# Who waits for the last store, and when: SyncE ahead of the engines' first meeting, or GpSimd after it

## The chip, the cores and the metric

The kernel runs on one core of a Trainium2 chip. The rounds of experiments ran on different chips (numbers 0, 5 and 14), so each ratio compares runs of one round alone. The time is device time in microseconds (us), and lower is better; the median of several executions is quoted. A profile belongs to one of these executions. Its span runs from the first to the last instruction of the program; what lies around the program is outside the span but inside the time (122.94 us of time for a span of 121.2 in the profiled run of the kernel before). After the program's last instruction the trace of that run has further semaphore updates: nine of semaphore 2 (121.389 to 121.914 us from the start of the span), a sweep over many others (121.813 to 122.479), and nine more of semaphore 2 (122.704 to 123.061). No instruction record names semaphore 2, so I put these updates down to the runtime, call semaphore 2 the runtime's and each group of nine a barrier; the names are mine.

## The reference

Two arrays of 1024 x 4096 floats are added, and GELU (in its tanh form) is taken of the sum:

```python
z = x + y
return (0.5 * z * (1 + np.tanh(np.sqrt(2 / np.pi) * (z + 0.044715 * z ** 3)))).astype(np.float32)
```

33.55 MB are read and 16.78 MB written: 50.3 MB for one pass of cheap arithmetic.

## The kernel before

The data lie on 128 partitions, 32768 floats on each. All ten loads and five stores are issued from SyncE's queue, the last two stores being half as large as the others (16 KB per partition). GpSimd adds, ScalarE and VectorE do the rest, in chunks of 1024 columns.

```python
    loads = [2048, 6144, 8192, 8192, 8192]
    stores = [8192, 8192, 8192, 4096, 4096]
    ...
    def store(i):
        a, b = sr[i]
        nc.sync.dma_start(out=ov[:, a:b], in_=zt[:, a:b])
    ...
    ctx.close()
    tc.close()
    tc.compile()
    begin_early(nc, 2)
```

The end that this case is about is not in the source: the framework adds it. It is the third block of the program, and its order is this (my summary of its instructions):

```
SyncE    drain: wait for all semaphores of the program (stores, loads, engines)
all      first meeting: four engines report (drain, semaphore 96 + 1);
         GpSimd waits for four reports, then lets them go (semaphore 97 + 4)
GpSimd   drain, clear of the program's semaphores 99 to 109
all      second meeting, like the first
```

In the trace instructions wait for a semaphore's value and change it: SyncE's drain at 120.466 us waits for semaphore 97 and raises 96, whose update follows at 120.474. Drains carry waits and reports here. ScalarE's first report, a drain, starts 6 ns after its last activation does (102.064 and 102.058 us), lasts 1.04 us and ends 35 ns after that activation (103.101 and 103.066); a later one lasts 14 ns. I call it a meeting when all engines report and are let go together. I count a transfer as landed at the 16th update of its semaphore: the last store makes 16, from 119.280 to 120.264 us, and SyncE's wait for it passes 17 ns after the last of them.

As I read this order, the first meeting is there so that no engine still needs a semaphore when they are cleared; the second, so that no engine leaves before they are. (`begin_early` moves the first two loads into the program's first block; both kernels have it.) SyncE's ten waits lie on six instructions in the trace, five semaphore instructions with one or two waits each and a drain with one. Semaphore 108 counts the last store (and one earlier load; its final value is 32).

Of the kernel before, what the change touches and what calls it, by code (L numbers as in the profile page):

```python
# [1 line left out]

# [1 line left out]

# [4 lines left out]


def begin_early(nc, count):


    blocks = nc.main_func.blocks
    head, body = blocks[0], blocks[1]
    SP = mybir.EngineType.SP
    queue = [i for i in body.instructions if i.engine == SP]
    moved = [i for i in queue if isinstance(i, mybir.InstDMACopy)][:count]
    assert not any(i.sync_info and i.sync_info.on_wait for i in moved)
    at = next(k for k, i in enumerate(head.instructions) if i.engine == SP and isinstance(i, mybir.InstDrain))  # L20
    for k, i in enumerate(moved):
        body.instructions.remove(i)
        head.instructions.insert(at + k, i)


@with_exitstack
def kernel(
    ctx: ExitStack,
    tc: tile.TileContext,
    x: bass.AP,  # L30
    y: bass.AP,
    out: bass.AP,
):








    nc = tc.nc
    P = nc.NUM_PARTITIONS
    fp32 = mybir.dt.float32
    act = mybir.ActivationFunctionType
    alu = mybir.AluOpType

    N, D = x.shape
    assert N % P == 0
    TOT = N // P * D  # L50
    xv, yv, ov = (a.rearrange("(p n) d -> p (n d)", p=P) for a in (x, y, out))

    c1 = 2.0 * math.sqrt(2.0 / math.pi)
    root = math.sqrt(c1 * 0.044715)

    YS = 8192
    CH = 1024
    PS = 4
    loads = [2048, 6144, 8192, 8192, 8192]
    stores = [8192, 8192, 8192, 4096, 4096]  # L60

    def ranges(sizes):
        ends = [sum(sizes[: i + 1]) for i in range(len(sizes))]
        assert ends[-1] == TOT
        return [(e - f, e) for e, f in zip(ends, sizes)]

    lr, sr, cr = ranges(loads), ranges(stores), ranges([CH] * (TOT // CH))
    C = len(cr)
    by_pool = set(range(1, C))

    def over(rs, lo, hi):
        return [i for i, (a, b) in enumerate(rs) if a < hi and b > lo]

    pool_sb = ctx.enter_context(tc.tile_pool(name="xz", bufs=1))
    pool_y = ctx.enter_context(tc.tile_pool(name="y", bufs=2))
    pool_w = ctx.enter_context(
        tc.tile_pool(name="w", bufs=PS, space=bass.MemoryType.PSUM)
    )

    zt = pool_sb.tile([P, TOT], fp32, tag="z", name="z")  # L80
    yt, wt = {}, {}

    def load_x(i):
        a, b = lr[i]
        nc.sync.dma_start(out=zt[:, a:b], in_=xv[:, a:b])  # L85

    def load_y(i):
        a, b = lr[i]
        s, o = divmod(a, YS)
        if o == 0:  # L90
            yt[s] = pool_y.tile([P, YS], fp32, tag="y", name=f"y{s}")
        nc.sync.dma_start(out=yt[s][:, o : o + b - a], in_=yv[:, a:b])  # L92
# [5 lines that stand above are left out]
    def add(c):  # L98
        a, b = cr[c]
        s, o = divmod(a, YS)  # L100
        eng = nc.gpsimd if c in by_pool else nc.vector
        eng.tensor_add(out=zt[:, a:b], in0=zt[:, a:b], in1=yt[s][:, o : o + b - a])  # L102

    def sq(c):
        a, b = cr[c]
        wt[c] = pool_w.tile([P, CH], fp32, tag="w", name=f"w{c}")
        nc.scalar.activation(  # L107
            out=wt[c], in_=zt[:, a:b], func=act.Square, scale=root
        )

    def stt(c):
        a, b = cr[c]
        nc.vector.scalar_tensor_tensor(  # L113
            out=wt[c], in0=wt[c], scalar=c1, in1=zt[:, a:b], op0=alu.add, op1=alu.mult
        )

    def sig(c):
        nc.scalar.activation(out=wt[c], in_=wt[c], func=act.Sigmoid)  # L118

    def mul(c):  # L120
        a, b = cr[c]
        nc.vector.tensor_mul(out=zt[:, a:b], in0=wt[c], in1=zt[:, a:b])  # L122


    sp = []
    for i in range(len(loads)):
        sp += [(load_x, i), (load_y, i)]
    sp += [(store, i) for i in range(len(stores))]
    pool = [(add, c) for c in range(C) if c in by_pool]
    dve, acts = [], []  # L130
    for i in range(-3, C + 1):
        if 0 <= i < C:
            dve.append((stt, i))
            acts.append((sig, i))
        if 0 <= i - 1 < C:
            dve.append((mul, i - 1))
        if 0 <= i + 3 < C and i + 3 not in by_pool:
            dve.append((add, i + 3))
        if 0 <= i + 2 < C:
            acts.append((sq, i + 2))  # L140

    needs = {
        load_x: lambda i: [],
        load_y: lambda i: [
            (add, c)
            for c in over(cr, lr[i][0] - 2 * YS, lr[i][0] - YS)
            if lr[i][0] % YS == 0
        ],
        add: lambda c: [(f, i) for i in over(lr, *cr[c]) for f in (load_x, load_y)],
        sq: lambda c: [(add, c)] + ([(mul, c - PS)] if c >= PS else []),  # L150
        stt: lambda c: [(sq, c)],
        sig: lambda c: [(stt, c)],
        mul: lambda c: [(sig, c)],
        store: lambda i: [(mul, c) for c in over(cr, *sr[i])],
    }
    queues = [sp, pool, acts, dve]
    done = set()
    with tc.manual_schedule():
        one = pool_sb.tile([P, 1], fp32, tag="one", name="one")
        nc.vector.memset(one, 0.0)  # L160
        nc.scalar.activation(out=one, in_=one, func=act.Sigmoid)  # L161
        while any(queues):
            moved = False
            for q in queues:
                while q and all(n in done for n in needs[q[0][0]](q[0][1])):
                    fn, arg = q.pop(0)
                    fn(arg)
                    done.add((fn, arg))
                    moved = True
                    if q is not sp:  # L170
                        break
            assert moved, [q[:1] for q in queues]

    ctx.close()
    tc.close()
    tc.compile()
    begin_early(nc, 2)


# [1 line left out]
_INS = ['x', 'y']  # L181
_OUTS = [((1024, 4096), 'float32')]


# [23 lines left out]
```

## Time and profile before

| | before |
|---|---|
| time, median (6 runs) | 122.67 us (122.49 to 123.08) |
| span of the profiled run | 121.2 us |
| transfers, mean over the span | 416 GB/s, 97.8% of 16 engines' time |
| last arithmetic ends | 104.3 us |
| last store, issue to landing | 15.91 us |

The first part of the page of the kernel before gives each engine's busy time, its share of the span and its number of instructions:

```profile
DVE 75.5 (62%) x66; ACT 63.8 (53%) x66; POOL 73.0 (60%) x35
```

No compute engine is busy for more than 62% of the span, while the transfer queue holds its 16 engines for 97.8% of it. The bound is memory traffic. What a change of the end can gain lies after the last store's landing. For that the page is too coarse, so the single records of instructions and semaphore updates are used below; they were read from the packed trace itself, since no view prints them, and have three decimals.

### The profile page before, as it was taken

To read this page: it belongs to the slowest core of one execution; us is meant where nothing else is said; L and a number is where in the kernel's file an instruction comes from. 1 tells how busy PE (TensorE), PEld (TensorE's weight loads), DVE (VectorE), ACT (ScalarE), POOL (GpSimd) and SP (SyncE) were. 2 spreads that over 40 slices of the span, in tenths; PEclk is the share of its full clock that TensorE was granted. 3 is DMA by queue.
4 is the path that set the end of the run, shared out by engine and by line. 5 is a ranking of instruction groups with operands and counts; after the bars stand their busy time and mean duration, and the time that the engine had idled before them with its cause. 6 is when DMAs were issued, how large, how long until landed. Compare 5 with 4: busy or idle time off the path is not lost.

```text
span 121.2 us, 248 instructions
## 1 busy us (share of the span) xinstructions
DVE 75.5 (62%) x66; ACT 63.8 (53%) x66; POOL 73.0 (60%) x35
## 2 busy tenths in 40 slices
DVE  0044700059999019999997999994999999400000
ACT  4016200078875047888858878874878878000000
POOL 0056000699980299999889999949999990000000
DMA  6999999999999989898989898998999999989992
GB/s 197 417 468 422 471 406 433 476 389 476 389 476 389 476 379 487 357 508 357 508 346 519 346 519 346 346 487 381 479 389 476 389 476 389 487 379 411 433 433 108
DMA packets 2162, 50.35 MB, mean 416 GB/s; under 512 B 240, under 2 KB 240, under 8 KB 240
## 3 DMA queue, kind: packets, MB, share of 16 engines
q1 hardware_dynamic: 2160, 50.33, 97.8%
q14 instruction: 2, 0.02, 0.0%
HBM read 33.55 MB, written 16.78 MB: 415 GB/s over the span
## 4 chain that ended last, share of the span: by engine, by line
DMA 49%; POOL 17%; DVE 16%; SPq 1%; ACT 1%; issue 0%; POOLq 0%
DMA y<-in_y_dram 49%; POOL z L102 17%; DVE z L122 8%; DVE w L113 8%; ACT w L107 1%; SPq L85 1%; SPq L92 1%; POOLq L102 0%
## 5 line engine op out<-in xcount | busy, mean ns | idle before, releaser
L102 POOL TENSOR_TENSOR z<-z,y 128x1024 f32<-128x1024 f32 x31 | 72.8, 2388 | 26.5 <-DMA y<-in_y_dram 26.5
L113 DVE SCALAR_TENSOR_TENSOR w<-w,z 128x1024 f32<-128x1024 f32 x32 | 39.4, 1232 | 21.4 <-ACT w L107 21.4
L107 ACT ACTIVATE w<-z 128x1024 f32<-128x1024 f32 x32 | 32.9, 1028 | 37.7 <-POOL z L102 31.7
L122 DVE TENSOR_TENSOR z<-w,z 128x1024 f32<-128x1024 f32 x32 | 38.8, 1214 | 0.0
L118 ACT ACTIVATE w<-w 128x1024 f32<-128x1024 f32 x32 | 31.4, 981 | 0.4 <-DVE w L113 0.4
L102 DVE TENSOR_TENSOR z<-z,y 128x1024 f32<-128x1024 f32 x1 | 1.2, 1224 | 6.1 <-DMA y<-in_y_dram 6.1
L161 ACT ACT_TABLE_LOAD x1 | 1.3, 1283 | 1.3 <-PEq L192 1.3
L160 DVE MEMSET one<- 128x1 f32 x1 | 0.1, 59 | 1.3 <-PEq L192 1.3
L192 POOL MEMSET const-float32-0.0<- 128x1 f32 x1 | 0.1, 99 | 0.2 <-issue 0.2
L161 ACT ACTIVATE one<-one 128x1 f32<-128x1 f32 x1 | 0.2, 203 | 0.0
L192 POOL MEMSET const-bfloat16-1.0<- 128x1 bf16 x1 | 0.1, 102 | 0.0
L192 POOL MEMSET const-uint8-127<- 128x1 uint8 x1 | 0.1, 102 | 0.0
L192 POOL MEMSET const-float32-1.0<- 128x1 f32 x1 | 0.1, 99 | 0.0
## 6 DMA issues: line engine op xcount, KB each, us to landing
z<-in_x_dram SPq DMA_DIRECT2D x3, 4096.0 KB, 34.2
y<-in_y_dram SPq DMA_DIRECT2D x3, 4096.0 KB, 24.8
out_dram<-z SPq DMA_DIRECT2D x3, 4096.0 KB, 30.8
out_dram<-z SPq DMA_DIRECT2D x2, 2048.0 KB, 17.5
z<-in_x_dram SPq DMA_DIRECT2D x1, 3072.0 KB, 13.4
y<-in_y_dram SPq DMA_DIRECT2D x1, 3072.0 KB, 20.4
z<-in_x_dram SPq DMA_DIRECT2D x1, 1024.0 KB, 4.9
y<-in_y_dram SPq DMA_DIRECT2D x1, 1024.0 KB, 6.9
```

The costliest lines, as they stand in the source:

```text
L85: nc.sync.dma_start(out=zt[:, a:b], in_=xv[:, a:b])
L92: nc.sync.dma_start(out=yt[s][:, o : o + b - a], in_=yv[:, a:b])
L102: eng.tensor_add(out=zt[:, a:b], in0=zt[:, a:b], in1=yt[s][:, o : o + b - a])
L107: nc.scalar.activation(out=wt[c], in_=zt[:, a:b], func=act.Square, scale=root)
L113: nc.vector.scalar_tensor_tensor(out=wt[c], in0=wt[c], scalar=c1, in1=zt[:, a:b], op0=alu.add, op1=alu.mult)
L118: nc.scalar.activation(out=wt[c], in_=wt[c], func=act.Sigmoid)
L122: nc.vector.tensor_mul(out=zt[:, a:b], in0=wt[c], in1=zt[:, a:b])
L160: nc.vector.memset(one, 0.0)
L161: nc.scalar.activation(out=one, in_=one, func=act.Sigmoid)
L192: nc = _bacc.Bacc("TRN2", target_bir_lowering=False, num_devices=1)
```

## The change

SyncE no longer waits for the last store ahead of the first meeting. The meeting then takes place while that store is under way, and GpSimd waits for the store afterwards, in the drain with which the clearing begins. The point is that the meeting does not need the store; only the clearing and the program's end do.

```diff
+def wait_late(nc):
+    body, end = nc.main_func.blocks[1:3]
+    SP, POOL = mybir.EngineType.SP, mybir.EngineType.Pool
+    last = [i for i in body.instructions if isinstance(i, mybir.InstDMACopy)][-1]
+    (sem,) = [u.id for u in last.sync_info.on_update]
+    all_done = end.instructions[0]
+    clear = next(i for i in end.instructions if isinstance(i, mybir.InstDrain) and i.is_reset_sema)
     ... (assertions)
+    waits = all_done.sync_info.on_wait
+    its = [w for w in waits if w.id == sem]
+    rest = [w for w in waits if w.id != sem]
+
+    def drain(old, waits, **reset):
+        return mybir.InstDrain(
+            name=old.name, engine=old.engine, debug=old.debug,
+            sync_info=mybir.SyncInfo(on_wait=waits, on_update=[]), **reset
+        )
+
+    at = end.instructions.index(clear)
+    end.instructions[0] = drain(all_done, rest, is_reset_sema=False)
+    end.instructions[at] = drain(
+        clear, its, is_reset_sema=True,
+        reset_range_start=clear.reset_range_start, reset_range_stop=clear.reset_range_stop,
+    )
 ...
     tc.compile()
     begin_early(nc, 2)
+    wait_late(nc)
```

More of the change, by code (lines that the diff above doesn't have):

```diff
@@ L23, in begin_early @@
         head.instructions.insert(at + k, i)
+def wait_late(nc):
[5 more added lines that the diff above has]
+    clear = next(i for i in end.instructions if isinstance(i, mybir.InstDrain) and i.is_reset_sema)
+    assert all_done.engine == SP and clear.engine == POOL and clear.sync_info is None
+    waits = all_done.sync_info.on_wait
+    its = [w for w in waits if w.id == sem]
+    assert len(its) == 1
+    rest = [w for w in waits if w.id != sem]
[10 more added lines that the diff above has]
+    )
 @with_exitstack
```

## The prediction

The sum came to 393 - 24 = 369 ns, all read off the trace of the kernel before, and so to 122.65 - 0.37 = 122.28 us.

> **What bounds the kernel now.** I read four views, from coarse to fine. First the page's slices of the span, to see what is at work when.
>
> ```profile
> DVE  0044700059999019999997999994999999400000
> ACT  4016200078875047888858878874878878000000
> POOL 0056000699980299999889999949999990000000
> DMA  6999999999999989898989898998999999989992
> GB/s 197 417 468 422 471 406 433 476 389 476 389 476 389 476 379 487 357 508 357 508 346 519 346 519 346 346 487 381 479 389 476 389 476 389 487 379 411 433 433 108
> ```
>
> The transfers are under way from the first slice to the last but one; the three compute engines are idle in the last five to seven slices (3.0 us each). So memory traffic bounds the kernel, and its end is set by the last store and whatever comes after it. The page's chain of work that ended last is of no use for this end: it follows arithmetic alone and stops with the last DVE multiply, at 104.3 us.
>
> Second, the windows view (busy time and transfer by stretch), over the last 2.2 us:
>
> ```profile
> 119.00:119.50 0.50, 0.00 (x0) 0.00 (x0) 0.00 (x0) 1.00 0.09 33
> 119.50:120.00 0.50, 0.00 (x0) 0.00 (x0) 0.00 (x0) 1.00 0.00 0
> 120.00:120.30 0.30, 0.00 (x0) 0.00 (x0) 0.00 (x0) 1.00 0.00 0
> 120.30:120.70 0.40, 0.00 (x0) 0.00 (x0) 0.00 (x0) 1.00 0.00 0
> 120.70:121.20 0.50, 0.00 (x0) 0.00 (x0) 0.00 (x0) 1.00 0.00 0
> ```
>
> The last two columns are the transfer share and GB/s, counted at a packet's start. No packet starts after 119.5 us, yet the span runs to 121.15: 1.6 us of end, in which neither data nor arithmetic is started.
>
> Third, the waits of the SyncE queue (total, times, longest):
>
> ```profile
> SPq L176 <- DMA out_dram<-z: 15.4, 3, 5.9
> SPq L176 <- PEq L176: 0.6, 2, 0.4
> ```
>
> Line 176 stands for everything the framework adds around the program. There SyncE waits three times for stores, 15.4 us in all: these are the last three stores, one after the other. What SyncE does after the third of those waits is the matter of the change.
>
> Fourth, line 176 alone, for GpSimd and for SyncE, from 120.3 and 104.7 us on (duration in ns min/median/max, first and last start):
>
> ```profile
> L176 POOLq EVENT_SEMAPHORE  x4: 17/17/17, 120.5 to 121.0; - x4
> L176 POOLq DRAIN  x2: 34/58/83, 120.7 to 120.9; - x2
> L176 POOLq EVENT_SEMAPHORE_RANGE_CLEAR  x1: 95/95/95, 120.8 to 120.8; - x1
> ...
> L176 SPq EVENT_SEMAPHORE  x7: 17/28/28, 104.7 to 121.1; - x7
> L176 SPq DRAIN  x3: 7/7/7, 120.4 to 120.7; - x3
> ```
>
> All four GpSimd semaphore instructions, both its drains and the clear fall after the last store. The individual records and semaphore updates behind these rows, to the nanosecond, give the order:
>
> | us | what |
> |---|---|
> | 115.437 | 16th update of the fourth store's semaphore |
> | 120.264 | 16th update of the last store's semaphore |
> | 120.281 | SyncE: wait for it and one older semaphore passes |
> | 120.342 | SyncE: next pair of waits, long fulfilled |
> | 120.407 | SyncE: the drain with the last wait, long fulfilled |
> | 120.466 | SyncE: drain that reports to the first meeting |
> | 120.498 | GpSimd: has seen all reports |
> | 120.576 | GpSimd: lets the others go |
> | 120.657 | GpSimd: drain (83 ns), first of the clearing |
> | 120.769 | GpSimd: clear of the semaphore range (95 ns) |
> | 120.893 | GpSimd: drain (34 ns) |
> | 120.971, 121.050 | GpSimd: second meeting, seen and let go |
> | 121.091 to 121.154 | the four other engines pass it; end of the span |
>
> So the end splits in three: last data packet over (119.887) to the semaphore's 16th update, 0.377 us; that update to GpSimd's first clearing drain, 120.657 - 120.264 = **0.393 us**; that drain to the end of the span, 121.154 - 120.657 = **0.497 us**.
>
> [...] SyncE's wait record is 28 ns long and starts 17 ns after the 16th update, though SyncE had stood there since 115.5 us. Hence I work from start to start, not with durations: the seven records from 120.281 to 120.657 last 7 to 83 ns, but their starts lie 32 to 81 ns apart. [...] The trace has 16 updates for the last store, from 119.280 to 120.264; whoever waits, GpSimd or SyncE, must wait for the one at 120.264. [...] The trace has updates of semaphore 2 from 121.389 on and a sweep of resets up to 122.48, all after the second meeting, so they should follow it as it moves.
>
> **The change part by part.**
>
> *Removed from SyncE:* the wait for the last store. Its remaining waits end with the fourth store's, at 115.437. Before, it took 120.466 - 120.264 = 0.202 us from the update to the report; after an equal sequence it reports near 115.437 + 0.2 = 115.64 (one pair of waits may fall away, 0.06 us). The other engines' reports are older: ACT's drain is at 102.06, DVE's at 103.11, its update at 104.39. GpSimd lets everyone go about 0.15 us later, near 115.8, and the four others report to the second meeting some 0.2 us after that (before: let go at 120.60, last report at 120.80), near 116.0. All this is 4.2 us ahead of the last store's landing, so all of it is hidden.
>
> *Moved to GpSimd:* the one wait, onto the first drain of the clearing. GpSimd will have stood there since about 115.9. It answers a semaphore that it has long waited for in 120.498 - 120.474 = 24 ns (its first-meeting wait in the kernel before, from update to start). So the drain starts at 120.264 + 0.024 = 120.288 instead of 120.657.
>
> *Unchanged:* drain, clear, drain, second meeting: 0.497 us. In the kernel before GpSimd was itself the last at the second meeting: the others' last report came at 120.801, while GpSimd's own second drain ended at 120.927. Earlier reports therefore gain nothing more there.
>
> Sum on the path: starts that leave it 17 + 61 + 65 + 59 + 32 + 78 + 81 = 393 ns; wait that comes onto it 24 ns; difference **0.369 us**. New span 121.154 - 0.369 = 120.785 us. The measured time has a further part around the span (122.94 against 121.2 in the profiled run) that I take to move along unchanged: 122.65 - 0.37 = **122.28 us**, 0.30% less.
>
> **The rivals.** *A: the wait costs an instruction more on GpSimd.* If the wait becomes a semaphore instruction of its own ahead of the drain, the path gets one more start-to-start step, 0.08 us by GpSimd's own (120.498 to 120.576 to 120.657). For it: SyncE's many waits were split into instructions of at most two. Against: SyncE's last drain carries one wait itself (120.407), and here too there is one wait. It would make 122.36. *B: nothing is gained, because something else already fills these 0.37 us,* such as the runtime's end work waiting for a transfer rather than for the engines. For it: the trace ends its program part at 121.154, and I can't see what the runtime waits for. Against: its first semaphore update comes 0.22 us after the second meeting's last, in an unbroken sequence. It would make 122.65. *C: more is gained, because the second meeting shrinks as well,* down to the full 0.89 us between landing and end of span. For it: the other engines arrive early. Against: 120.801 is before 120.927, GpSimd was the last anyway, and the clear can't start before the store has landed. With everything gone it would make 121.76, still within 2%[...]. *D: the store lands later,* because SyncE or the meeting disturbs it. Against: these are a few semaphore updates at 115.6 to 116.0 beside 433 GB/s, and the kernel before passes like updates at 104.39 and 110.6. No change of time that I could name.
>
> **Range and chances.** The three runs before lie within 0.20 us (122.49 to 122.69), and transfers set the time, so a median of a new session may lie 0.1 to 0.25 us off without any change. The gain has a narrow range by itself (0.29 with rival A to 0.39). Both together: 121.98 to 122.57 for 8 in 10; this leaves B's 122.65 just outside, to which I give one chance in ten. Two per cent is 2.45 us, while the whole end after the landing, all that a rearrangement of the engines could remove, is 0.89 us: faster by over 2% 0.005, slower 0.005, within 0.99.
>
> **What would show each step.** In the changed kernel's records: (i) SyncE's report to the first meeting and GpSimd's letting go lie 4 us or more before the last store's 16th update, near 115.6 and 115.8; (ii) GpSimd's 83 ns drain starts within 30 ns of that update (about 0.1 with rival A); (iii) from that drain to the end of the span 0.49 to 0.50 us; (iv) from the update to the end of the span 0.52 us instead of 0.89; (v) the store takes 15.9 us from issue to landing, as before. The prediction would be wrong if (ii) shows over 0.1 us, if (iii) has grown (GpSimd slower after a wait), or if all five hold and the time still doesn't fall by 0.3 to 0.4 us against runs of the kernel before on the same chip: then the rest of the time doesn't move with the span.

## The result

The changed kernel takes 122.27 us (median of 6 runs, 121.96 to 122.44) against 122.67 us. The ratio is 0.9963, with a 95% interval of 0.9942 to 0.9984. Ratios here are the mean time of one kernel's runs over that of the other's of the same rounds, so not quite the ratio of the medians that I quote. The interval leaves out 1, so there is a small gain.

**The profile after.** The transfer lines of its slices (40 equal slices of the span; busy share in tenths, then GB/s):

```profile
DMA  6999999989898989898989899999999999998994
GB/s 201 430 457 449 440 416 446 468 381 489 348 522 348 522 348 522 348 511 359 500 370 489 381 478 391 359 402 459 394 468 402 468 402 468 391 478 364 430 435 174
```

The picture is the same up to the last slice, which now is 4 tenths full instead of 2: the idle end is a smaller part of it. The windows view of the changed kernel over its last 1.5 us (start and end, length, busy time of VectorE, ScalarE and GpSimd, clock, transfer share, GB/s):

```profile
119.00:119.50 0.50, 0.00 (x0) 0.00 (x0) 0.00 (x0) 1.00 0.08 33
119.50:120.00 0.50, 0.00 (x0) 0.00 (x0) 0.00 (x0) 1.00 0.00 0
120.00:120.30 0.30, 0.00 (x0) 0.00 (x0) 0.00 (x0) 1.00 0.00 0
120.30:120.53 0.23, 0.00 (x0) 0.00 (x0) 0.00 (x0) 1.00 0.00 0
```

As before, no packet of data starts after 119.5 us (the trace has a packet of 4 bytes at 119.629, and before two at 119.523 and 119.883, which the view shows as 0 GB/s and the prediction left out); but the span ends at 120.53 instead of 121.15. The waits of SyncE's queue (total, times, longest), where line 205 of this kernel is line 176 of the one before:

```profile
SPq L205 <- DMA out_dram<-z: 10.6, 2, 5.8
SPq L205 <- PEq L205: 5.0, 2, 4.9
```

SyncE waits for two stores instead of three. In place of the third wait (4.8 us) stands a wait of 4.9 us for other engines: SyncE now spends the last store's time standing at the second meeting. Line 205 in the changed kernel, first GpSimd from 115.0 to 115.6 us, then GpSimd from 119.5 us on, then SyncE from 104.3 us on:

```profile
L205 POOLq EVENT_SEMAPHORE  x2: 17/17/17, 115.4 to 115.5; - x2
...
L205 POOLq DRAIN  x2: 34/58/83, 120.0 to 120.3; - x2
L205 POOLq EVENT_SEMAPHORE  x2: 17/17/17, 120.4 to 120.4; - x2
L205 POOLq EVENT_SEMAPHORE_RANGE_CLEAR  x1: 95/95/95, 120.1 to 120.1; - x1
...
L205 SPq EVENT_SEMAPHORE  x6: 17/28/28, 104.6 to 120.5; - x6
L205 SPq DRAIN  x3: 7/7/7, 115.3 to 115.6; - x3
```

GpSimd's four semaphore instructions, which all stood behind the last store, have come apart: the first meeting's two lie at 115.4 and 115.5 us, the second's two at 120.4. SyncE's three drains have gone from 120.4 to 120.7 us to 115.3 to 115.6. The durations are the same. One of SyncE's semaphore instructions is gone, because the nine waits left lie on five instructions, two on each of four and one on the drain, where the ten lay on six.

The single records of the two traces side by side (us from the start of each span):

| event | before | after |
|---|---|---|
| fourth store, 16th update | 115.437 | 115.193 |
| SyncE reports to the first meeting | 120.466 | 115.396 |
| GpSimd lets the others go | 120.576 | 115.507 |
| last store, 16th update | 120.264 | 120.013 |
| GpSimd's first clearing drain starts | 120.657 | 120.037 |
| end of the span | 121.154 | 120.534 |
| last update of the runtime's semaphore 2 | 123.061 | 122.442 |
| last store's update to that drain | 0.393 | 0.024 |
| that drain to the end of the span | 0.497 | 0.497 |
| end of the span to the runtime's last update | 1.907 | 1.908 |

Where the 0.620 us between the two spans came from: 0.369 us from the distance between the landing and the drain, nothing from what follows, and the remaining 0.251 us because the store landed earlier in this execution. Of these, 0.244 us were there already when the fourth store landed (115.193 against 115.437), ahead of the first meeting and with all stores issued, so they are hardly the change's. Several of the experiments bear on it.

### The profile page after: what moved, and what is told of

Same layout as the page of the kernel before. It is cut to its first block, busy times and chain, and to the rows that moved or that the text cites. A ratio compares the mean times of both kernels' runs of the same rounds, so it can differ in the third digit from the quotient of the medians.

```text
span 120.5 us, 247 instructions
## 1 busy us (share of the span) xinstructions
DVE 75.5 (63%) x66; ACT 63.8 (53%) x66; POOL 73.0 (61%) x35
## 4 chain that ended last, share of the span: by engine, by line
DMA 49%; POOL 17%; DVE 16%; SPq 1%; ACT 1%; issue 0%; POOLq 0%
DMA y<-in_y_dram 49%; POOL z L131 17%; DVE z L151 8%; DVE w L142 8%; ACT w L136 1%; SPq L114 1%; SPq L121 0%; POOLq L131 0%
```

## The experiments

My theory is the prediction's: between the last store's 16th semaphore update and the end of the span, the starts of instructions that follow each other add up one by one, and what is moved ahead of that update is free. The rivals: it counts who waits and not when the meeting is held; the store itself lands earlier or later; something beside the engines' end sets the time.

All of these kernels gave correct results. Their edits are shown shortened, with parts in words. The distance from the last store's 16th update to the end of the span is called **the tail** from here on. It was 0.890 us before and 0.521 us after, and it comes from one profile of each kernel. The scatter of the runs, about 0.2 us either way, comes mostly from elsewhere, as the comparison further down shows.

### Only the order of SyncE's waits

```diff
     waits = old.sync_info.on_wait
+    waits = [w for w in waits if w.id == sem] + [w for w in waits if w.id != sem]
```

(The first wait of the list ends up in the drain itself, the last of SyncE's six instructions.)

> SyncE still waits for all stores ahead of the first meeting, but for the last one last of all, in the drain that carries one wait itself. Theory (only starts between the last store's 16th semaphore update and the end of the span count): two starts of 61 and 65 ns leave that path, so update to end of span falls from 0.890 to 0.764 us and the time by 0.13 us, about a third of the change's gain. Rival 1 (the gain needs the store to be waited for after the meeting; the order of waits is nothing): 0.89 us and no gain. Rival 2 (the changed kernel gained because its store landed earlier, 120.01 against 120.26 us in its profile): update to end as the theory has it, but the landing moves in step with the number of SyncE's waits, so here as in the kernel before, near 120.26.

Measured: tail **0.764 us** (119.949 to 120.713), time 122.45 against 122.61 us, ratio 0.9986 (0.9965 to 1.0008). SyncE's waits and its records from 119 us on:

```profile
SPq L190 <- DMA out_dram<-z: 15.3, 3, 5.8
...
L190 SPq DRAIN  x3: 7/7/7, 120.0 to 120.3; - x3
L190 SPq EVENT_SEMAPHORE  x2: 17/17/17, 120.2 to 120.7; - x2
```

SyncE still waits for three stores. After the landing there are only drains, reports and the meetings' own semaphore instructions; the two instructions with waits long fulfilled that stood there before, the pair at 120.342 and the drain's own at 120.407, no longer follow the last store's wait, which the drain now carries. The tail is the theory's, to the nanosecond, so rival 1 falls: 0.126 of the 0.369 us have nothing to do with when the meeting is held. They are two instructions whose waits were fulfilled and that happened to stand behind the last store's. The landing is 0.32 us earlier than in the kernel before although SyncE has the same number of waits, which speaks against rival 2; it is one execution of each, and the comparison further down has more on it. The time's interval includes both 0 and 0.13 us; the timer alone would not have told.

### GpSimd waits, but ahead of the first meeting

```diff
+    end.instructions[0] = drain(old, rest)      # SyncE: without the last store's
+    end.instructions[at] = drain(first, its)    # GpSimd's drain ahead of the first meeting
```

> GpSimd instead of SyncE waits for the last store, but ahead of the first meeting, so the meeting still comes after the landing. Theory: SyncE's report (0.202 us after the update) leaves the path; GpSimd's answer to the store (24 ns), one more start-to-start step of GpSimd (78 to 112 ns), its release (78) and the step to the clearing drain (81) stay: 0.26 to 0.30 us from the update to that drain instead of 0.393, update to end of span 0.76 to 0.79, time 0.10 to 0.13 us less. Rival 1 (it is who waits that counts, not when the meeting is): update to end near 0.52 and the whole gain of 0.37.

Measured: tail **0.759 us** (119.732 to 120.491), time 122.44 against 122.61 us, ratio 0.9984 (0.9962 to 1.0007). GpSimd's records from 119.5 to 120.06 us:

```profile
L202 POOLq DRAIN  x2: 41/59/77, 119.8 to 120.0; - x2
L202 POOLq EVENT_SEMAPHORE  x2: 17/17/17, 119.8 to 119.9; - x2
```

GpSimd's drain starts 24 ns after the update, as in the changed kernel; its semaphore instruction follows 85 ns later (41 ns drain), the release 78 ns after that, the clearing drain 81 ns after that. Having GpSimd wait is worth 0.131 us (of which 6 ns are a clearing drain of 77 instead of 83 ns) and not 0.369. The other 0.238 us of the change come from holding the meeting before the landing.

### One meeting more, before and after the change

```diff
+    meeting = list(end.instructions)[1:at]      # the 11 instructions of the first meeting
+    for k, i in enumerate(meeting):
+        end.instructions.insert(at + k, <a copy of i under a new name>)
```

> The kernel before with the first meeting held twice. Theory: after the first release the others report at up to 144 ns later than GpSimd's drain starts, so GpSimd sees the reports of the added meeting 0.33 us after the first's (120.825 for 120.498): update to end of span 1.22 us instead of 0.89, time 0.33 us more. Rival (what the engines do at the end is hidden beside something else that ends the timed run): no change of the time though the span grows.

> The changed kernel with the first meeting held twice. Theory: the added 0.33 us lies beside the store, from about 115.4 us on, and costs nothing: update to end of span stays 0.52 us, time as the changed kernel (0.37 us under the kernel before). Rival (meetings cost wherever they stand, for instance by disturbing the store): 0.33 us of the gain is lost, so nearly the time of the kernel before, or the store lands later by a like amount.

Measured, before with three meetings: tail **1.212 us**, that is 0.322 us more; time 122.70 against 122.61 us, ratio 1.0005 (0.9987 to 1.0024). After with three meetings: tail **0.515 us**; time 122.16 against 122.61 us, ratio 0.9958 (0.9940 to 0.9975).

The tails are as expected (the clearing drain took 77 instead of 83 ns, which is the 6 ns in both). The time of the first is not: 0.33 us more were expected, and the interval ends at 0.29. Either its executions happened to have early landings, or the meetings don't count in full. So the dose was raised.

### Eight meetings more

The same edit with the copied meeting eight times.

> The kernel before with the first meeting held nine times (ten meetings in all). One added meeting took 0.322 us more from landing to end of span in its profile, but its timed runs showed only about 0.1 us, within their scatter; eight added ones are out of the scatter. Theory: 8 x 0.328 = 2.62 us more on the path, update to end of span 3.51 us, time near 125.25 us. Rival (the time is bound by something beside the engines' end, and the meetings are partly hidden): the span grows, the time by less than half of 2.62.

> The changed kernel with the same eight added meetings. Theory: they end near 115.6 + 2.6 = 118.2 us, 1.8 us ahead of the last store's landing, so update to end of span stays 0.515 us and the time stays near 122.25. Rival (meetings disturb the store, or cost wherever they stand): the store's 15.8 us from issue to landing, or the time, grows by a good part of 2.6 us.

Measured, before with ten meetings: tail 3.804 us, 2.914 more than before; time 125.88 against 122.81 us, ratio 1.0252 (1.0235 to 1.0268). After with ten meetings: tail **0.519 us**; time 122.47 against 122.81 us, ratio 0.9976 (0.9960 to 0.9992). The records of GpSimd from 120.3 us on in the first:

```profile
L196 POOLq EVENT_SEMAPHORE  x20: 17/17/17, 120.6 to 124.0; - x20
L196 POOLq DRAIN  x10: 34/34/77, 120.7 to 123.9; - x10
L196 POOLq EVENT_SEMAPHORE_RANGE_CLEAR  x1: 95/95/95, 123.8 to 123.8; - x1
```

and in the second, first from 115.0 to 118.6 us, then from 119.9 us on:

```profile
L225 POOLq EVENT_SEMAPHORE  x18: 17/17/17, 115.5 to 118.5; - x18
L225 POOLq DRAIN  x8: 34/34/41, 115.6 to 118.2; - x8
...
L225 POOLq DRAIN  x2: 34/56/77, 120.1 to 120.3; - x2
L225 POOLq EVENT_SEMAPHORE  x2: 17/17/17, 120.4 to 120.5; - x2
L225 POOLq EVENT_SEMAPHORE_RANGE_CLEAR  x1: 93/93/93, 120.2 to 120.2; - x1
```

These are the same instructions. In the one kernel all twenty semaphore instructions stand behind the landing (120.343 us) and the clear comes at 123.8; in the other, eighteen stand beside the store and the clear comes at 120.2, as if they weren't there. The time follows: the first takes 3.07 us more than the kernel before (difference of the medians), the second is still 0.34 us below it. Its store took 15.78 us from issue to landing, so eight meetings beside it did not slow it. So the engines' end counts in full. That run's missing 0.24 us (0.09 measured for 0.33) lie within the span: the record has the span of each execution to 0.1 us, and time less span is 1.8 us there as in the kernel before, while the median spans are 120.9 and 121.0 us. Nothing is hidden in the runtime's part. Earlier landings in those executions would explain it; their landings are not on record. The profiled one, at 123.02 us, was the slowest of the six.

The tail came out 0.29 us longer than expected in the first kernel. Seven of the eight meetings took 0.327 to 0.367 us from start to start; one took 0.575, and it was the seventh added one in all three of the long kernels. In that one the last report came at 122.885 us and GpSimd started 271 ns later instead of 24. The long kernels have one more packet in their instruction queue; here the one made from the kernel before (packets, MB, share of 16 engines' span):

```profile
q14 instruction: 3, 0.02, 0.1%
```

It was 2 before. It would be tempting to say that GpSimd waited for that packet, but the trace speaks against it: the packet starts at 123.831 us, 0.675 us after GpSimd had gone on (123.156), and in the two longer forms of the changed kernel 1.0 and 1.4 us after the slow meeting. What GpSimd waited for stays open.

### More meetings than fit

The changed kernel with twenty meetings added, in one execution.

> The changed kernel with twenty added meetings, more than fit beside the store. Theory (GpSimd's clearing starts at the later of two times: the landing, and the end of the meetings): the meetings end at 115.59 + 20 x 0.328 = 122.15 us, 2.1 us after a landing at 120.0; update to end of span 2.6 us, time near 124.4. Rival (the clearing only waits for the store, or the time doesn't follow): time near 122.3, or up by all of 6.6 us.

Measured: tail 2.938 us, time 125.22 us. The clear, from GpSimd's records after the landing:

```profile
L225 POOLq EVENT_SEMAPHORE_RANGE_CLEAR  x1: 96/96/96, 122.8 to 122.8; - x1
```

GpSimd's clearing drain starts at 122.680 us, though the store had landed at 120.240: the meetings had not ended before. Expected were 122.15 us for the drain and a tail of 2.6. The drain is 0.53 us late: 0.17 because the stores ran later here (SyncE's report at 115.568 instead of 115.396), 0.25 from the slow seventh meeting, and about 0.1 from three of 0.36 us instead of 0.33. The time is 0.8 us over the expected 124.4: 0.34 from the tail, 0.24 from the later landing, and about 0.26 that no recorded update accounts for (see the comparison of times below). The rule holds for the drain, its size was a little low: the clearing starts at the later of two times, the landing and the end of the meetings, and what can be hidden is limited to the 4.4 us between GpSimd's being ready and the landing (115.59 to 120.01 in the changed kernel).

### Everything but one wait ahead of the landing

If a meeting that doesn't need the store is free beside it (tail 0.519 us with eight more of them, 0.521 with none), so should be the second meeting and the clearing of all semaphores but one. The next kernel does that. The clear covers semaphores 99 to 107; GpSimd takes 16 off semaphore 109 with a semaphore instruction; both meetings are held; and the last instruction of the whole program waits for the store's semaphore to be 32 and subtracts 32 in the same instruction.

```diff
+    end.instructions[0] = drain(all_done, rest, is_reset_sema=False)       # without the last store
+    end.instructions[at] = drain(clear, [], is_reset_sema=True, reset_range_start=lo, reset_range_stop=sem)
+    end.instructions[at + 1] = shorter                                     # clear of 99 to 107
+    end.instructions.insert(at + 2, wait_and_take_off("I-9000", POOL, above[0]))   # 109
     ... second meeting, unchanged
+    end.instructions.append(wait_and_take_off("I-9100", <engine>, its[0])) # 108, the last store
```

> A step further than the change: all semaphores but the last store's are cleared, and the second meeting is held, while the store is under way; at the very end GpSimd alone waits for the store and subtracts its 32 in the same instruction. Theory: 24 ns to GpSimd's answer and 17 ns of it are left in the program, 0.04 us instead of 0.521; if the runtime's 1.907 us after the span follow as one piece, update to the last of the runtime's semaphore updates 1.95 us instead of 2.43, time 0.48 us under the changed kernel and 0.85 under before, near 121.8. Rival 1 (the other engines, already in the runtime's own barrier, have part of it done): still less, as much as 0.2 to 0.5 us. Rival 2 (the runtime waits by other means for transfers or for all engines' records): no gain over the changed kernel.

Measured: tail **0.041 us**, time 121.84 against 122.81 us, ratio 0.9932 (0.9914 to 0.9950). By the ratio that is 0.84 us under before, where 0.85 was expected. From the landing to the runtime's last update it took 2.037 us instead of the 1.95 expected (2.429 after the change), so rival 2 falls. The program's part is as the theory has it; the runtime's part grew from 1.908 to 1.996 us. The updates of the runtime's semaphore 2 say why:

| kernel | first of its barriers after the program, updates in us |
|---|---|
| after | 120.769, 120.803, **121.008**, 121.052, 121.075, then four up to 121.294 |
| all ahead, GpSimd last | 116.417, 116.451, **120.617**, 120.662, 120.685, then four up to 120.903 |

Two updates come while the store is still under way, the third only after GpSimd is done. So the updates are a chain, and GpSimd is third in it. In both kernels the third update comes 0.561 us after the end of GpSimd's last instruction (120.447 and 120.056 us). In the changed kernel the other engines leave the second meeting up to 87 ns after GpSimd, so the end of the span was never the point from which the runtime's part should have been counted: GpSimd's own end was. With that, 0.480 us of shorter tail less 0.087 is 0.393 us, and the measured gain from landing to the runtime's end is 0.392.

This also says that 0.561 us between GpSimd's last instruction and its place in the chain lie on the path in all kernels so far. Another engine might have less.

### The same with another engine last

> As the run before in which all the end but one wait lies beside the store, but SyncE has that last wait. There GpSimd's first update of the runtime's semaphore came 0.561 us after its last instruction, as in all kernels so far, with two updates ahead of it already at 116.4 us: the runtime's barrier is a chain with GpSimd third in it, and its 0.561 us of its own lie on the path. Theory: with another engine last, that falls off, and SyncE's own time up to its update is like that of the chain's first engine (0.235 us after the end of the span): update of the store to last update of the runtime's semaphore 1.65 to 1.85 us instead of 2.04, time 0.2 to 0.4 us under that run, near 121.5. Rival (each engine has some 0.56 us of its own ahead of that barrier): 2.0 us, time as with GpSimd.

> The same with the last wait on ScalarE. Theory: its place in the runtime's chain decides: if its update is among the first two (those that came at 116.4 us when GpSimd was last), more of the chain is still ahead of it than with an engine that comes after GpSimd, by some 0.1 us. 1.75 to 1.9 us from the store's update to the runtime's last; time 0.1 to 0.3 us under the run with GpSimd. Rival as for SyncE: 2.0 us.

> The same with the last wait on VectorE. Theory: 1.65 to 1.85 us from the store's update to the runtime's last, according to its place in the chain. Rival: 2.0 us.

> The same with the last wait on TensorE, whose semaphore instructions take 51 ns where the others' take 17 to 21. Theory: 1.75 to 1.9 us from the store's update to the runtime's last, if it is early in the chain. Rival: 2.0 us.

Measured (against the same runs of before, 122.75 us, but for the row of GpSimd, which is of the round before, against 122.81; "own" is from the end of the engine's last instruction to its update of semaphore 2, "rest" from there to the runtime's last update):

| last engine | updates ahead of it | tail | own | rest | landing to runtime's end | time, us | ratio, 95% |
|---|---|---|---|---|---|---|---|
| TensorE | 0 | 0.080 | 0.274 | 1.505 | 1.859 | 121.63 | 0.9914 (0.9901 to 0.9928) |
| ScalarE | 1 | 0.039 | 0.139 | 1.472 | 1.650 | 121.51 | 0.9904 (0.9890 to 0.9917) |
| GpSimd (run before) | 2 | 0.041 | 0.561 | 1.435 | 2.037 | 121.84 | 0.9932 (0.9914 to 0.9950) |
| VectorE | 3 | 0.049 | 0.183 | 1.388 | 1.620 | 121.43 | 0.9900 (0.9886 to 0.9914) |
| SyncE | 4 | 0.034 | 0.140 | 1.313 | 1.487 | 121.35 | 0.9893 (0.9876 to 0.9909) |

Line 232 in the run with SyncE last, first all engines from 117 us on, then GpSimd from 114 us on:

```profile
L232 SPq EVENT_SEMAPHORE  x1: 17/17/17, 119.9 to 119.9; - x1
...
L232 POOLq EVENT_SEMAPHORE  x5: 17/17/17, 115.3 to 115.9; - x5
L232 POOLq DRAIN  x2: 34/55/76, 115.4 to 115.8; - x2
L232 POOLq EVENT_SEMAPHORE_RANGE_CLEAR  x1: 92/92/92, 115.5 to 115.5; - x1
```

One semaphore instruction of 17 ns is all that the program still does after 117 us. The rival (0.56 us for each engine) falls: it is GpSimd's alone. The number of updates ahead gives the order of the chain directly: TensorE, ScalarE, GpSimd, VectorE, SyncE. The later an engine stands in it, the less is left behind it: the "rest" falls from 1.505 to 1.313 us. SyncE stands last and has next to the shortest time of its own, so it is the right one. Its 1.487 us, and those of ScalarE and VectorE, lie below what I had expected, because I took each engine's own time to be like TensorE's 0.235 us; it was 0.14 to 0.18.

With SyncE last the kernel takes **121.35 us**, 1.1% less than before and 0.7% less than the changed kernel, if the two ratios to before are compared (0.9893 and 0.9963; they are not of the same rounds).

### Does the time follow?

From the landing to the runtime's last update, in each profile, against the median time:

| kernel | landing to runtime's end | time | time less it |
|---|---|---|---|
| before | 2.797 | 122.67 | 119.87 |
| order of waits only | 2.670 | 122.45 | 119.78 |
| GpSimd ahead of the meeting | 2.665 | 122.44 | 119.78 |
| before, 3 meetings | 3.121 | 122.70 | 119.58 |
| before, 10 meetings | 5.712 | 125.88 | 120.17 |
| after | 2.429 | 122.27 | 119.84 |
| after, 3 meetings | 2.417 | 122.16 | 119.74 |
| after, 10 meetings | 2.422 | 122.47 | 120.05 |
| all ahead, GpSimd | 2.037 | 121.84 | 119.80 |
| all ahead, SyncE | 1.487 | 121.35 | 119.86 |

The end differs by 4.2 us between these kernels, and what is left after taking it off lies between 119.6 and 120.2. The before of the round with ten meetings was itself at 122.81, against 122.67 and 122.61 in the two earlier rounds, which explains a part of the 120.17 and 120.05. The 119.58 of the kernel before with three meetings is the one that stands apart; as said above, its missing time lies within the span.

Within one execution the match is much closer. In all 13 kernels with timed rounds the time of the profiled execution is 0.117 to 0.128 us less than the runtime's last update, counted from the start of the span (before: 122.94 and 123.061; after: 122.32 and 122.442), over ends that differ by 4.2 us. Only the single execution with twenty added meetings falls out: its time is 0.139 us more than that update (125.22 and 125.081), and why stays open.

So the time is the landing plus the end, and the landing scatters. In the profiles of the kernels that keep SyncE's wait for all stores it lay at 120.264, 119.949, 120.027 and 120.343 us; in the one in which GpSimd waits ahead of the meeting at 119.732; in those of the changed kernel and its three longer forms at 120.013, 119.927, 120.046 and 120.240; with all ahead between 119.874 and 120.155. The groups overlap. The 0.251 us by which the store landed earlier in the changed kernel's profile are within this scatter, and the medians show no earlier landing: what is left in the table is 119.87 us for before and 119.84 for after.

## Why the prediction was right

**The path and its sum.** Right, step by step. The 393 ns of seven starts became 24 ns, the answer that I had read off GpSimd's wait at the first meeting. The tail was predicted as 0.52 us and is 0.521. The runs split the 0.369 us further than the prediction did: 0.126 us are SyncE's two instructions with fulfilled waits, which a mere reordering also takes off the path; 0.243 us are the report, the meeting and the step to the clearing drain.

**What is hidden.** Right. SyncE's report comes 0.203 us after the fourth store's update (0.202 predicted); the clock times 115.64 and 115.8 were 0.24 and 0.29 us late, 0.244 of it because the fourth store landed that much earlier in this execution. The rest of the second is a misreading: the prediction took 0.15 us from the report to the letting go, where its own table has 0.110 (120.466 to 120.576); it was 0.111 after. None of it is on the path. The second reports came at 115.65 to 115.73, 4.3 us ahead of the landing. That they cost nothing was shown by adding eight more meetings to them.

**What is unchanged.** 0.497 us from the drain to the end of the span, in both. No further gain came from the others' early reports, as predicted.

**The rivals.** A (an instruction more) did not happen: the one wait stayed in the drain, at 24 ns. B (something else fills the time) falls with the two kernels of ten meetings: 2.9 us added on the path cost 3.07 us, the same work beside the store cost nothing. C (more is gained) did not happen in this change, but its idea is sound if the second meeting is moved as well, and a further 0.9 us (0.94 from the landing to the runtime's end) between the changed kernel and the one with SyncE last came from there and from the runtime's chain. D (the store is disturbed) did not happen: 15.82 us from issue to landing, 15.91 before.

**The part around the span.** I took it to move along unchanged; it did, 1.907 and 1.908 us. Against rival B I had read the first update, 0.22 us after the second meeting, as the next step of the path; the step on the path is the third update, GpSimd's. That cost nothing here. I had not seen what the runtime's part follows: not the end of the span but GpSimd's own last instruction, 87 ns earlier, and 0.561 us of GpSimd's after it.

**The time.** 122.27 us for 122.28 predicted. That they agree to 0.01 us is luck: the six runs lie 0.48 us apart. The measured ratio allows a gain of 0.20 to 0.71 us. What shows the size of 0.37 us is the trace, not the timer.

## What to carry to other kernels

When a kernel ends with a wait for a transfer, list everything that comes after that transfer's semaphore and ask of each instruction whether it needs the data; what doesn't need it goes ahead of the wait (0.369 us of tail here, 0.890 to 0.521), and fulfilled waits go ahead of the one that isn't (0.126 us of that). Then try which engine does best with the last wait: here it was SyncE, with 1.487 us from the landing to the runtime's last update, against 2.037 with GpSimd. SyncE had 0.140 us of its own up to its update of semaphore 2, fifth in the chain, and GpSimd 0.561, third. The gains here were 0.37 us for the change and 1.31 with SyncE last (2.797 to 1.487); I read them from the distances within the trace, because the six runs of the changed kernel lie 0.48 us apart. All of this was shown on one kernel.
